# The last two rows of the last chunk but one, stored by indirect transfers from GpSimd

## The chip, the cores and the metric

The kernel runs on one core of a Trainium2 chip. The time is device microseconds of one execution. Before the change the median of three runs is 1331.59 us (1331.28 to 1331.63). A profile is one execution recorded on the chip.

## The reference

`logits` has shape (2, 8, 2112, 2112), `rel_bias` (8, 33), both float32.

```python
pos = np.arange(S)
rel = pos[:, None] - pos[None, :]
rel_clipped = np.clip(rel, -max_rel, max_rel) + max_rel        # max_rel = 16
bias = rel_bias[:, rel_clipped]
logits = logits + bias[None, :, :, :]
logits = logits - logits.max(axis=-1, keepdims=True)
exp = np.exp(logits)
return exp / exp.sum(axis=-1, keepdims=True)
```

A bias that depends only on the clipped distance between row and column is added, and a softmax is taken along each row of 2112. The input is 285 MB and so is the output.

## The kernel before

The 2 x 8 x 2112 = 33,792 rows are laid over the 128 partitions, 264 neighbouring rows to each. A chunk is six rows of every partition (`R = 6`), 128 x 50,688 bytes; there are 44 chunks, numbered 0 to 43 here, and four buffers `X[0]` to `X[3]` (`NBUF = 4`), used in turn. Chunk 42, the last but one, lies in `X[2]`.

At the start a table `M` of the bias against distance is built in PSUM; `strip` copies the stretch of it that four chunks need into `F`. For each row of a chunk VectorE adds the bias and finds the negated maximum (`add`, L181), ScalarE takes the exponential and its sum (`exps`, L190), and VectorE takes the reciprocals of three rows and scales them (`scale`, L198 and L202), in place. Each engine runs its own loop over chunks, and semaphores tie them: `ld[b]` says that buffer b is loaded, `scaled` counts rows that are done, `st[b]` that the store has landed. `take` waits for a count and takes it off again.

All big transfers are issued by SP, in one queue (q1 in the profile). Its loop stores a chunk when six rows of it are scaled (`store`, L93), waits until the store of the buffer before has landed, and loads the next chunk there (`load`, L89). A transfer of 128 partitions is spread over the core's 16 DMA engines, eight partitions to each.

Chunk 0 is stored in another way. Its first five rows go as one transfer (L219). The sixth goes as 17 small ones, the "fan" (L223), with 15, 14, 13, ... 1 partitions, which cover the 128 partitions between them. A transfer of k ≤ 15 partitions puts one on each of k DMA engines, so the fan loads them unequally. GpSimd waits for all of these (`main`, `fan[0]`, `fan[1]`) and then sets `st[0]`, which SP awaits in its loop.

After the loop SP stores chunks 41 and 42 whole and chunk 43 in two halves of three rows (semaphore `landed`). It waits for the remaining `st` and, at the very end of the program (L244), for `landed`.

Of the kernel before, what the change touches and what calls it, by code (L numbers as in the profile page):

```python
# [8 lines left out]
I32 = mybir.dt.int32  # L9
EXP = mybir.ActivationFunctionType.Exp  # L10
ALU = mybir.AluOpType
# [4 lines left out]
def kernel(  # L16
# [6 lines left out]
    nc = tc.nc  # L23
    P = 128
    B, H, S, S2 = logits.shape
# [3 lines left out]
    ROWS = B * H * S // P  # L29
    PB = S // ROWS  # L30
    assert ROWS * P == B * H * S and PB * ROWS == S and PB == H == 8
    R = 6
    NBUF = 4
    STEP = R * NBUF
    N = ROWS // R
# [2 lines left out]
    MW = S + ROWS - 1  # L38
    FW = S + STEP - 1
    BIG = 3.0e38  # L40
    LANES = 9
    FAN = []
    for lane in range(LANES):
        m = len(range(lane, P, LANES))
        k = 15 if lane == 0 else 15 - lane
# [4 lines left out]
    io = ctx.enter_context(tc.tile_pool(name="io", bufs=1))  # L50
    X = [io.tile([P, R * S], FP32, tag=f"X{b}", name=f"X{b}") for b in range(NBUF)]
# [2 lines left out]
    nmax = io.tile([P, STEP], FP32, tag="nmax", name="nmax")  # L54
    tot = io.tile([P, STEP], FP32, tag="tot", name="tot")
    rec = io.tile([P, STEP], FP32, tag="rec", name="rec")
    ip = io.tile([P, 3, PB], I32, tag="ip", name="ip")
    ps = ctx.enter_context(tc.tile_pool(name="ps", bufs=1, space=bass.MemoryType.PSUM))
    M = ps.tile([P, 4096], FP32, tag="M", name="M")

    def view(t, offset, dims):

        return bass.AP(tensor=t.tensor, offset=t.offset + offset, ap=[[list(t.ap[0])[0], P]] + dims)

    def rows(t, j, n):

        return bass.AP(tensor=t.tensor, offset=t.offset + j * S, ap=[[ROWS * S, P], [1, n * S]])

    with tc.tile_critical(no_gpsimd_drain=True):
        ld = [nc.alloc_semaphore(f"ld{b}") for b in range(NBUF)]  # L70
        st = [nc.alloc_semaphore(f"st{b}") for b in range(NBUF)]
        added = nc.alloc_semaphore("added")
        expd = nc.alloc_semaphore("expd")
        scaled = nc.alloc_semaphore("scaled")
# [2 lines left out]
        pre = nc.alloc_semaphore("pre")  # L77
        idx = nc.alloc_semaphore("idx")
        dve = nc.alloc_semaphore("dve")
        main = nc.alloc_semaphore("main")  # L80
        fan = [nc.alloc_semaphore(f"fan{i}") for i in range(2)]
        landed = tc.alloc_semaphore("landed")

        def take(eng, sem, n):
            eng.wait_ge(sem, n).then_inc(sem, -n)  # L85


        def load(j, b):
            nc.sync.dma_start(out=X[b][:, :], in_=rows(logits, j, R)).then_inc(ld[b], 16)  # L89

        def store(j, b, s0=0, n=R, sem=None):
            take(nc.sync, scaled, n)
            nc.sync.dma_start(  # L93
                out=rows(out, j + s0, n), in_=X[b][:, s0 * S : (s0 + n) * S]
            ).then_inc(sem or st[b], 16)


        for r in range(R):
            nc.sync.dma_start(
                out=X[0][:, r * S : (r + 1) * S], in_=rows(logits, r, 1)  # L100
            ).then_inc(ld[0] if r == R - 1 else pre, 16)
        for n in range(1, NBUF):
# [6 lines left out]
            out=rbB,  # L109
            in_=bass.AP(tensor=rel_bias.tensor, offset=rel_bias.offset, ap=[[0, P], [1, H * W]]),  # L110
        ).then_inc(rb, 16)
        nc.gpsimd.iota(ip[:, 0], pattern=[[0, PB]], base=0, channel_multiplier=1).then_inc(idx, 1)
        nc.gpsimd.iota(ip[:, 2], pattern=[[1, PB]], base=0, channel_multiplier=0).then_inc(idx, 1)  # L113
        take(nc.gpsimd, main, 16)
        take(nc.gpsimd, fan[0], 16 * ((len(FAN) + 1) // 2))
        take(nc.gpsimd, fan[1], 16 * (len(FAN) // 2))
        nc.gpsimd.sem_inc(st[0], 16)

        v = nc.vector
        done = [0]  # L120
# [21 lines left out]
        for m, op in ((eq, ALU.is_equal), (gt, ALU.is_gt), (le, ALU.is_le), (lt, ALU.is_lt)):  # L142
# [4 lines left out]
            out=view(F, 0, [[W, H], [1, W]]), in0=view(F, 0, [[W, H], [1, W]]),  # L147
# [3 lines left out]
                             axis=mybir.AxisListType.X, op=ALU.add))  # L151
# [5 lines left out]
            out=view(F, 0, [[W, PB], [1, W]]), in0=view(F, SC + 2 * PB, [[1, PB], [0, W]]),  # L157
# [7 lines left out]
            out=view(M, U, [[ROWS, PB], [1, W]]), in0=view(F, 0, [[W, PB], [1, W]]),  # L165
            in1=view(F, SC + 8 * PB, [[1, PB], [0, W]]), op=ALU.add))
        then(v.tensor_copy(out=view(M, U + W, [[ROWS, PB], [1, ROWS - W]]),  # L167
                           in_=view(F, SC + 7 * PB, [[1, PB], [0, ROWS - W]])))
# [8 lines left out]
        def add(b):  # L177
            take(v, ld[b], 16)
            for r in range(b * R, (b + 1) * R):
                x = X[b][:, (r - b * R) * S : (r - b * R + 1) * S]  # L180
                v.tensor_tensor_reduce(  # L181
                    out=x, in0=x, in1=F[:, STEP - 1 - r : STEP - 1 - r + S], scale=-1.0, scalar=BIG,
                    op0=ALU.add, op1=ALU.min, accum_out=nmax[:, r : r + 1],
# [37 lines left out]
        for i, (k, g, lane) in enumerate(FAN):  # L221
            p = g * LANES + lane
            nc.sync.dma_start(  # L223
                out=bass.AP(
                    tensor=out.tensor, offset=out.offset + (p * ROWS + R - 1) * S,
                    ap=[[LANES * ROWS * S, k], [1, S]],
                ),
                in_=bass.AP(
                    tensor=X[0].tensor, offset=X[0].offset + p * PSX + (R - 1) * S,
                    ap=[[LANES * PSX, k], [1, S]],  # L230
                ),
            ).then_inc(fan[i % 2], 16)
        with nc.Fori(0, ROWS - 2 * STEP + 1, STEP, engines=[ENG.SP]) as j:
            for b in range(NBUF):
                store(j + (b + 1) * R, (b + 1) % NBUF)
                take(nc.sync, st[b], 16)
                load(j + (b + NBUF) * R, b)
        for n in range(N - NBUF + 1, N - 1):
            store(n * R, n % NBUF)
        store((N - 1) * R, (N - 1) % NBUF, 0, HALF, landed)  # L240
        store((N - 1) * R, (N - 1) % NBUF, HALF, R - HALF, landed)
        for b in range(NBUF - 1):
            take(nc.sync, st[(N + b) % NBUF], 16)
    nc.sync.wait_ge(landed, nc.sync.to_reg(32), synchronizes=[nc.sync.lower_ap(out)])  # L244


# [28 lines left out]
```

## Time and profile before

| | |
|---|---|
| median of three runs | 1331.59 us |
| profiled execution | 1331.3 us |
| its span, first to last instruction | 1329.5 us |
| VectorE busy | 976.7 us, 73% |
| ScalarE busy | 575.2 us, 43% |
| GpSimd busy | 0.4 us |
| bytes moved | 285.61 MB read, 285.47 MB written, 430 GB/s over the span |

The page divides the span into 40 slices and gives each engine's busy tenths; the DMA row is the mean of the core's 16 DMA engines. A view of stretches gives the same between any two times. In it the last two numbers of a row are the DMA share and the GB/s, and the one before them is the granted clock of TensorE, which this kernel doesn't use. Issue times of transfers stand in the timeline of SP, with a q behind the engine's name for its queue of issues; when a transfer lands is given as a median by kind.

### The profile page before, as it was taken

To read this page: it belongs to the slowest core of one execution; us is meant where nothing else is said; L and a number is where in the kernel's file an instruction comes from. 1 tells how busy PE (TensorE), PEld (TensorE's weight loads), DVE (VectorE), ACT (ScalarE), POOL (GpSimd) and SP (SyncE) were. 2 spreads that over 40 slices of the span, in tenths; PEclk is the share of its full clock that TensorE was granted. 3 is DMA by queue.
4 is the path that set the end of the run, shared out by engine and by line. 5 is a ranking of instruction groups with operands and counts; after the bars stand their busy time and mean duration, and the time that the engine had idled before them with its cause. 6 is when DMAs were issued, how large, how long until landed. Compare 5 with 4: busy or idle time off the path is not lost. (4 is left out here: it accounts for less than half of the span.)

```text
span 1329.5 us, 2477 instructions
## 1 busy us (share of the span) xinstructions
DVE 976.7 (73%) x911; ACT 575.2 (43%) x539; POOL 0.4 (0%) x6
## 2 busy tenths in 40 slices
DVE  5998767777877776787778767677877776687772
ACT  2565333444444343345444333444444343345440
POOL 0000000000000000000000000000000000000000
DMA  9999999999999999999999999999999999999997
GB/s 391 427 426 424 436 430 433 438 433 435 432 435 435 433 436 430 436 433 435 430 433 439 433 433 427 439 435 432 433 432 438 430 433 430 436 430 436 438 432 337
DMA packets 13939, 571.12 MB, mean 430 GB/s; under 512 B 1648, under 2 KB 1776, under 8 KB 1776
## 3 DMA queue, kind: packets, MB, share of 16 engines
q1 hardware_dynamic: 13792, 570.96, 99.5%
q10 hardware_dynamic: 144, 0.14, 0.1%
q14 instruction: 3, 0.02, 0.0%
HBM read 285.61 MB, written 285.47 MB: 430 GB/s over the span
## 5 line engine op out<-in xcount | busy, mean ns | idle before, releaser
L181 DVE CUSTOM_DVE_ANT_0 X<-X,F 128x2112 f32<-128x2112 f32 x264 | 605.2, 2354 | 302.0 <-DVEq L85 302.0
L190 ACT ACTIVATE X<-X,nmax 128x2112 f32<-128x2112 f32 x264 | 541.7, 2052 | 538.2 <-ACTq L85 516.4
L202 DVE TENSOR_SCALAR X<-X,rec 128x2112 f32<-128x2112 f32 x264 | 332.5, 1316 | 13.2
L190 ACT ACT_TABLE_LOAD x11 | 14.1, 1283 | 185.8 <-ACTq L85 185.8
L190 ACT ACTIVATION_READ_ACCUMULATOR X<-X,nmax 128x1 f32 x264 | 49.2, 186 | 0.0
L175 DVE COPY F<-M 128x2135 f32 x11 | 26.1, 2375 | 6.6 <-DVEq L85 6.6
L181 DVE DVE_READ_ACCUMULATOR2_ANT nmax<- 128x1 f32 x264 | 21.7, 82 | 0.0
L198 DVE RECIPROCAL rec<-tot 128x3 f32<-128x3 f32 x88 | 15.0, 170 | 0.0
L146 DVE TENSOR_TENSOR F<-F 128x264 f32<-128x264 f32 x1 | 0.4, 435 | 4.9 <-DMA F<-in_rel_bias_dram 4.9
L167 DVE COPY M<-F 128x1848 f32<-128x1848 f32 x1 | 2.1, 2077 | 0.0
L133 DVE TENSOR_SCALAR ip<-ip 128x8 int32<-128x8 int32 x1 | 0.2, 172 | 1.3 <-POOL ip L113 1.3
L150 DVE TENSOR_REDUCE rbS<-F 128x33 f32<-128x264 f32 x1 | 0.6, 610 | 0.0
L164 DVE TENSOR_TENSOR M<-F 128x264 f32<-128x264 f32 x1 | 0.4, 441 | 0.0
L156 DVE TENSOR_TENSOR F<-F,rbS 128x264 f32<-128x264 f32 x1 | 0.4, 426 | 0.0
L143 DVE TENSOR_SCALAR F<-F 128x8 f32<-128x8 f32 x4 | 0.4, 167 | 0.0
L169 DVE COPY M<-rbS 128x247 f32<-128x247 f32 x1 | 0.4, 406 | 0.0
L154 DVE TENSOR_SCALAR F<-F,rbS 128x8 f32<-128x8 f32 x1 | 0.2, 231 | 0.0
L160 DVE SCALAR_TENSOR_TENSOR F<-F,rbS 128x8 f32<-128x8 f32 x1 | 0.2, 227 | 0.0
L155 DVE TENSOR_SCALAR F<-F,rbS 128x8 f32<-128x8 f32 x1 | 0.2, 225 | 0.0
L161 DVE SCALAR_TENSOR_TENSOR F<-F,rbS 128x8 f32<-128x8 f32 x1 | 0.2, 221 | 0.0
L136 DVE TENSOR_TENSOR F<-ip 128x8 f32<-128x8 int32 x1 | 0.2, 167 | 0.0
L139 DVE TENSOR_TENSOR F<-ip 128x8 f32<-128x8 int32 x1 | 0.2, 167 | 0.0
(9 smaller groups left out, 1.2 us busy)
## 6 DMA issues: line engine op xcount, KB each, us to landing
X<-in_logits_dram SPq DMA_DIRECT2D x43, 6336.0 KB, 44.7
out_dram<-X SPq DMA_DIRECT2D x42, 6336.0 KB, 52.8
X<-in_logits_dram SPq DMA_DIRECT2D x6, 1056.0 KB, 12.6
out_dram<-X SPq DMA_DIRECT2D x2, 3168.0 KB, 21.9
out_dram<-X SPq DMA_DIRECT2D x1, 5280.0 KB, 34.9
F<-in_rel_bias_dram ACTq DMA_DIRECT2D x1, 132.0 KB, 6.4
out_dram<-X SPq DMA_DIRECT2D x1, 123.8 KB
out_dram<-X SPq DMA_DIRECT2D x1, 115.5 KB
```

The lines of the kernel that those rows point to most:

```text
L143: then(v.tensor_scalar(out=m, in0=dp, scalar1=0.0, scalar2=None, op0=op))
L146: then(v.tensor_tensor(out=view(F, 0, [[W, H], [1, W]]), in0=view(F, 0, [[W, H], [1, W]]), in1=view(F, SC + 3 * PB, [[1, H], [0, W]]), op= ...
L150: then(v.tensor_reduce(out=rbS[:, :], in_=view(F, 0, [[1, W], [W, H]]), axis=mybir.AxisListType.X, op=ALU.add))
L156: then(v.tensor_tensor(out=view(F, 0, [[W, PB], [1, W]]), in0=view(F, SC + 2 * PB, [[1, PB], [0, W]]), in1=view(rbS, W - 1, [[0, PB], [-1, ...
L164: then(v.tensor_tensor(out=view(M, U, [[ROWS, PB], [1, W]]), in0=view(F, 0, [[W, PB], [1, W]]), in1=view(F, SC + 8 * PB, [[1, PB], [0, W]] ...
L167: then(v.tensor_copy(out=view(M, U + W, [[ROWS, PB], [1, ROWS - W]]), in_=view(F, SC + 7 * PB, [[1, PB], [0, ROWS - W]])))
L169: then(v.tensor_copy(out=M[:, 0:U], in_=low.to_broadcast([P, U])))
L175: v.tensor_copy(out=F[:, :], in_=M[:, bass.ds(ROWS - STEP - j, FW)]).then_inc(dve, 1)
L181: v.tensor_tensor_reduce(out=x, in0=x, in1=F[:, STEP - 1 - r : STEP - 1 - r + S], scale=-1.0, scalar=BIG, op0=ALU.add, op1=ALU.min, accum_ ...
L190: nc.scalar.activation(out=x, in_=x, func=EXP, scale=-1.0, bias=nmax[:, r : r + 1], accum_out=tot[:, r : r + 1],).then_inc(expd, 1)
L198: v.reciprocal(out=rec[:, r0 : r0 + HALF], in_=tot[:, r0 : r0 + HALF]).then_inc(inv, 1)
L202: v.tensor_scalar_mul(out=x, in0=x, scalar1=rec[:, r : r + 1]).then_inc(scaled, 1)
```

## The change

SP's store of chunk 42 is cut to its first four rows (`R - PAIR`). The last two rows of every partition, 2 x 2112 x 4 = 16,896 bytes that are neighbours in memory, are stored by GpSimd in six indirect transfers. Seen so, `out` is a table of 16,896 such pairs, and partition p's pair of chunk 42 has number 132 p + 128.

`PLAN` lists the six as (n, p0, a, b). Each transfer reads n partitions from p0 on, and takes its n targets from a column of the new tile `sel`. The column holds the pair numbers of partitions p0 to p0 + n - 1, with those outside the kept range a to b - 1 replaced by a number past the end of `out` (`FAR`), which an indirect transfer with `oob_is_err=False` skips. The kept ranges cover 0 to 127 once. The six lists name 16 + 16 + 16 + 48 + 48 + 112 = 256 partitions and keep 128.

GpSimd fills the columns at the start with 6 iotas and 12 selects, each waiting for the one before through the semaphore `pool`. It issues the transfers after a wait for `ready`, which SP sets when it has counted the six scaled rows of chunk 42, just ahead of its own shorter store. They count on the semaphore `soft`, awaited at the end of the program ahead of `landed`.

```diff
+    PLAN = [(16, 1, 12, 17), (16, 10, 17, 20), (16, 20, 20, 24), (48, 0, 0, 12), (48, 6, 24, 51), (112, 16, 51, 128)]
+    PAIR = 2
+    FAR = 1 << 20
...
+    sel = io.tile([P, len(PLAN)], I32, tag="sel", name="sel")
...
+        g = nc.gpsimd
+        BLK = ROWS // PAIR
+        AT = ((N - 1) * R - PAIR) // PAIR
...
+        for w, (n, p0, a, b) in enumerate(PLAN):
+            col = sel[:, w : w + 1]
+            step(g.iota(col, pattern=[[0, 1]], base=p0 * BLK + AT, channel_multiplier=BLK))
+            for base, mul in ((p0 - a, 1), (b - 1 - p0, -1)):
+                g.wait_ge(pool, made[0])
+                step(g.affine_select(out=col, in_=col, pattern=[[0, 1]], base=base, channel_multiplier=mul,
+                                     compare_op=ALU.is_ge, fill=float(FAR)))
+        take(g, pool, made[0])
         take(nc.gpsimd, main, 16)
         take(nc.gpsimd, fan[0], 16 * ((len(FAN) + 1) // 2))
         take(nc.gpsimd, fan[1], 16 * (len(FAN) // 2))
         nc.gpsimd.sem_inc(st[0], 16)
+        take(g, ready, 1)
+        pairs = out.rearrange("b h s t -> (b h s t)").rearrange("(n c) -> n c", c=PAIR * S)
+        late = X[(N - 2) % NBUF]
+        lap = list(late.ap[0])[0]
+        for w, (n, p0, a, b) in enumerate(PLAN):
+            g.indirect_dma_start(
+                out=pairs, out_offset=bass.IndirectOffsetOnAxis(ap=sel[0:n, w : w + 1], axis=0),
+                in_=bass.AP(tensor=late.tensor, offset=late.offset + p0 * lap + (R - PAIR) * S,
+                            ap=[[lap, n], [1, PAIR * S]]),
+                in_offset=None, bounds_check=B * H * S // PAIR - 1, oob_is_err=False,
+            ).then_inc(soft, 16)
...
-        for n in range(N - NBUF + 1, N - 1):
+        for n in range(N - NBUF + 1, N - 2):
             store(n * R, n % NBUF)
+        take(nc.sync, scaled, R)
+        nc.sync.sem_inc(ready, 1)
+        nc.sync.dma_start(
+            out=rows(out, (N - 2) * R, R - PAIR), in_=X[(N - 2) % NBUF][:, 0 : (R - PAIR) * S]
+        ).then_inc(st[(N - 2) % NBUF], 16)
...
+    nc.sync.wait_ge(soft, nc.sync.to_reg(16 * len(PLAN)), synchronizes=[nc.sync.lower_ap(out)])
     nc.sync.wait_ge(landed, nc.sync.to_reg(32), synchronizes=[nc.sync.lower_ap(out)])
```

More of the change, by code (lines that the diff above doesn't have):

```diff
@@ L40 @@
     BIG = 3.0e38
+    PLAN = [(16, 1, 12, 17), (16, 10, 17, 20), (16, 20, 20, 24), (48, 0, 0, 12), (48, 6, 24, 51), (112, 16, 51, 128)]
+    PAIR = 2
+    FAR = 1 << 20
+    assert sorted(p for n, p0, a, b in PLAN for p in range(a, b)) == list(range(P))
     LANES = 9
@@ L79 @@
         dve = nc.alloc_semaphore("dve")
+        ready = nc.alloc_semaphore("ready")
+        pool = nc.alloc_semaphore("pool")
+        soft = tc.alloc_semaphore("soft")
         main = nc.alloc_semaphore("main")
@@ L113, with step @@
         nc.gpsimd.iota(ip[:, 2], pattern=[[1, PB]], base=0, channel_multiplier=0).then_inc(idx, 1)
+        g = nc.gpsimd
+        BLK = ROWS // PAIR
+        AT = ((N - 1) * R - PAIR) // PAIR
+        made = [0]
+        def step(ins):
+            made[0] += 1
+            ins.then_inc(pool, 1)
+        for w, (n, p0, a, b) in enumerate(PLAN):
[6 more added lines that the diff above has]
+        take(g, pool, made[0])
         take(nc.gpsimd, main, 16)
```

## The prediction

> **What bounds the kernel.** The page first: its span, busy lines, slices and queues.
>
> ```profile
> span 1329.5 us, 2477 instructions
> DVE 976.7 (73%) x911; ACT 575.2 (43%) x539; POOL 0.4 (0%) x6
> DMA  9999999999999999999999999999999999999997
> ...
> q1 hardware_dynamic: 13792, 570.96, 99.5%
> q10 hardware_dynamic: 144, 0.14, 0.1%
> q14 instruction: 3, 0.02, 0.0%
> ```
>
> VectorE works 73% of the span and ScalarE 43%, but the DMA row reads nine tenths or more in 39 slices and 7 in the last. One queue, SP's q1, carries 99.5% of 16 engines' span. The kernel moves 571 MB as fast as its 16 DMA engines take it; only the start and that last slice leave them idle. The second view is stretches of time, for the DMA share (next to last column) and the GB/s.
>
> ```profile
> 78.00:1300.00 1222.00, 907.90 (x836) 538.82 (x506) 0.00 (x0) 1.00 1.00 433
> ...
> 1320.00:1321.00 1.00, 0.00 (x0) 0.00 (x0) 0.00 (x0) 1.00 0.77 329
> 1321.00:1322.00 1.00, 0.00 (x0) 0.00 (x0) 0.00 (x0) 1.00 0.59 253
> 1322.00:1323.00 1.00, 0.00 (x0) 0.00 (x0) 0.00 (x0) 1.00 0.41 177
> 1323.00:1324.00 1.00, 0.00 (x0) 0.00 (x0) 0.00 (x0) 1.00 0.41 177
> 1324.00:1325.00 1.00, 0.00 (x0) 0.00 (x0) 0.00 (x0) 1.00 0.24 101
> 1325.00:1326.00 1.00, 0.00 (x0) 0.00 (x0) 0.00 (x0) 1.00 0.18 76
> 1326.00:1327.00 1.00, 0.00 (x0) 0.00 (x0) 0.00 (x0) 1.00 0.06 25
> 1327.00:1328.00 1.00, 0.00 (x0) 0.00 (x0) 0.00 (x0) 1.00 0.06 25
> 1328.00:1329.50 1.50, 0.00 (x0) 0.00 (x0) 0.00 (x0) 1.00 0.00 0
> ```
>
> The share falls in sixteenths: three DMA engines at 1325, one alone (0.06) from 1326 to 1328. From 78 to 1300 us each engine moved 433 / 16 = 27.1 GB/s; the one left alone moves 25 by packets that start in the stretch, so no faster. The limit is per engine, and the time is set by the engine with the most left. The shares from 1320 on sum to 2.72 us of all sixteen. A packet counts where it starts, and one of 25,344 B lasts 0.94 us at 27.1 GB/s, so half of that is added: evenly shared, the work would end at 1320 + 2.72 + 0.47 = 1323.2. The last packet ends at 1328.1. **At most 4.9 us can be won by sharing the tail out.** Third, what the tail waits for: SP's waits, its issues, and the transfers by line (last column: median us from issue to landing).
>
> ```profile
> SPq L244 <- DMA out_dram<-X: 14.6, 1, 14.6
> ...
> 1238.15 0.35 SPq L89 DMA_DIRECT2D X<-in_logits_dram  x1
> 1244.93 60.38 SPq L93 DMA_DIRECT2D out_dram<-X  x4
> ...
> X<-in_logits_dram SPq DMA_DIRECT2D x43, 6336.0 KB, 44.7
> out_dram<-X SPq DMA_DIRECT2D x42, 6336.0 KB, 52.8
> out_dram<-X SPq DMA_DIRECT2D x2, 3168.0 KB, 21.9
> ```
>
> SP's last wait is for stores alone. A chunk's store lands 52.8 us after its issue though moving it takes 6.49 MB / 433 GB/s = 15 us: the queue is long, and a store issued a few us later starts no later.
>
> **Which DMA engine is late.** No view names engines. I followed the single packet records behind these rows: on one engine a packet starts a few ns before its predecessor ends. The fan of chunk 0 labels them, taking k ≤ 15 rows a transfer: engine 0 gets 17 rows, 1 to 6 get 15, 14, 13, 12, 11, 10, down to none on 15, against 8 if even. So read, the last packets end: engine 4 at 1328.1, engines 0 to 3 at 1324.6 to 1326.2, engine 5 at 1324.2, 6 to 8 at 1321.7 to 1322.3, the others at 1320.9 to 1322.0, save one at 1324.1, which I read as 10 or 15 and cannot settle. Engine 4 is no heir of the fan alone; its packets run about 0.4% long all through.
>
> **The change, part by part.**
>
> *The dealing.* Chunk 42 loses two of six rows from SP's store. They go as 128 pieces (two rows of a partition, 16,896 B), 16,896 / 27.1 = 0.62 us each. Before, each engine had 8. I take a list of n rows to be dealt in blocks of n/16: 7, 3 or 1 to an engine. Every kept range begins and ends on such a block (51 - 16 = 35 = 5 x 7; 24 - 6 = 18 = 6 x 3; 12 = 4 x 3). That gives engines 0 to 3 four pieces, 4 none, 5 seven, 6 and 10 ten, 7 to 9 and 11 to 14 eleven, 15 eight. Engine 4: -8 x 0.62 = -5.0, end 1323.1. Engines 0 to 3: -2.5, ends 1322.1 to 1323.7. Engine 5: -0.6, 1323.6. Engine 6: +1.25, 1323.6. Those with eleven: +1.9, 1322.8 to 1323.8. The odd one, if 15, stays at 1324.1; if 10, it goes to 1325.3. I take 15, since then all sixteen come within 2 us. Latest 1324.1 for 1328.1: **-4.0 us** (bounds -4.3 and -2.8).
>
> *Smaller pieces and six more completions per engine.* 11 pieces and 6 tokens at a few ns: +0.1 us.
>
> *Two queues on one DMA engine.* Before has no indirect transfer. The nearest rows are the start, where ACT's q10 (1,056 B packets) runs between SP's packets:
>
> ```profile
> 4.00:5.50 1.50, 0.00 (x0) 0.00 (x0) 0.00 (x0) 1.00 0.91 234
> 5.50:7.00 1.50, 0.00 (x0) 0.00 (x0) 0.00 (x0) 1.00 0.94 363
> 7.00:9.50 2.50, 2.00 (x7) 0.00 (x0) 0.00 (x0) 1.00 1.02 433
> ```
>
> Mixed with the first reads, the rate is 234, but in the packet records from 5.6 to 6.7 us single q10 packets of 47 ns stand between q1 packets at their usual 319 ns: 0 to 0.04 us a change. The other end is q14's instruction packet at 1310.6, behind which a q1 packet took 0.28 us too long. I take 0.02 x 11 = +0.2 us, nearest to two data queues; the upper end is 0.28 x 11 = 3.1.
>
> *Generation on GpSimd.* `ready` comes when chunk 42 is scaled:
>
> ```profile
> 1271.08 3.78 DVE L202 TENSOR_SCALAR X<-X,rec 128x2112 f32<-128x2112 f32 x3
> 1283.08 2.36 DVE L181 CUSTOM_DVE_ANT_0 X<-X,F 128x2112 f32<-128x2112 f32 x1 [8.22 <-DVEq L85]
> ...
> 1301.09 3.78 DVE L202 TENSOR_SCALAR X<-X,rec 128x2112 f32<-128x2112 f32 x3
> ...
> 44.01 12.37 SPq L223 DMA_DIRECT2D out_dram<-X  x17
> ```
>
> That is 1274.9; the queue is busy until 1320. Generation has 45 us of cover. SP's 17 small transfers issued in 12.4 us, so six take at least 6 x 0.73 = 4.4 us there; no row bounds GpSimd from above. I cost it at nothing; past the cover each us counts. The rows mostly land where SP's store did, so chunk 43's load (issued 1238.15, awaited at 1283.08) may be pushed by about a piece or two (1.2 us). Its first store half is issued when the run of 1297.08 ends, at 1300.9, and chunk 42's store lands only about 1306; cover 3 us, nothing on the path.
>
> *The lists.* 6 iotas and 12 selects on GpSimd at the start, before its wait for the first stores:
>
> ```profile
> 1.13 0.14 POOL L113 IOTA ip<- 128x8 int32 x1
> ...
> 19.04 2.38 DVE L175 COPY F<-M 128x2135 f32 x1 [6.58 <-DVEq L85]
> ```
>
> 18 x 0.14 plus a semaphore each is about 6 us; the wait behind them opens only at 78 us (the fan is issued at 44 to 56). [...] Nothing.
>
> *The ends.* SP waits for `soft` ahead of `landed`: the rows were issued 26 us before the last store, nothing. `soft` lies apart from the other cleared semaphores, so GpSimd clears twice; the whole stretch after the last packet is 1.4 us (1328.1 to 1329.5), one clear more +0.2 (bounds 0 and 1).
>
> Sum: -4.0 + 0.1 + 0.2 + 0.2 = **-3.5 us**. The profiled execution took 1331.3 (1.8 around its span): 1327.8. The median of the runs is 0.3 higher, 1331.59, so **1328.1**.
>
> [...]
>
> **Rivals.**
>
> 1. *The dealing is another* (piece i on engine i mod 16, or skipped pieces closed up before dealing). Modulo gives 7 to 9 pieces everywhere, engine 4 still 8, and the end stays: 1331.6 + 0.5 = 1332.1. For it: no list of before shows how GpSimd deals. Against: the ranges fall on blocks.
> 2. *Changing queues costs as behind q14.* 0.28 us a piece: engines 7 to 14 at up to 1323.8 + 3.1 = 1326.9, a gain of 1.2 less 0.3: 1330.7. From 0.37 us a piece nothing is left.
> 3. *Skipped pieces move all the same (slower).* The lists name 256 pieces and keep 128. If a skipped one occupies its engine like a kept one, each engine carries 16 for 8: +8 x 0.62 = 5.0 us, engine 4 too: 1331.6 + 5.0 + 0.5 = 1337.1. It decides once a skipped piece costs 0.45 of a kept one, since engine 4 skips sixteen (16 x 0.62 x 0.45 = 4.5, back at 1327.6). Nothing in before speaks for or against.
> 4. *GpSimd is late.* VectorE scales from 1297.08 to 1304.9. If generation cannot work beside VectorE and misses the 8.22 us gap, the last list (7 pieces, 4.4 us an engine) comes after 1305: still hidden. Only past about 1318 does it cost: at 1325, 1325 + 4.4 + 1.4 = 1330.8 of span, about 1333. [...]
>
> **How the numbers follow.** Forecast 0.56: the blocks account for every bound in the plan and the ends meet. Rival 1: 0.12 (0.09 within, 0.03 slower). Rival 2: 0.12 (0.10 within, 0.02 slower). Rival 3: 0.11. Rival 4: 0.05 (0.01 within, 0.04 slower). A setup cost that no row here shows: 0.04 slower. A change under 0.2%, 2.7 us, can hardly be told from none. Faster 0.56, same 0.20, slower 0.24. The forecast's own range is 1327.0 (nearly the whole 4.9 us) to 1329.5 (10 late, changes at 0.1 us). For 8 in 10 it reaches over rivals 1, 2 and part of 4, to 1333.5.
>
> **What would show it.** The end of the tail: shares staying near 1.0 until about 1322 and gone by 1324.5. q1 short of 2.16 MB, which another queue carries. Bytes unchanged (else rival 3). GpSimd's six transfers issued between 1275 and 1290. Wrong would be one engine alone for 2 us again (rival 1), or a share below 1 while both queues have work (rival 2).

## The result, and the profile after

The change made the kernel slower: 1337.38 us, the median of five runs (1336.70 to 1337.63), against 1331.34 us for the kernel before in runs beside it (1331.28 to 1331.63). The ratio is 1.0044, with a 95% interval from 1.0030 to 1.0059. The prediction was 1328.1 us in a range from 1327.0 to 1333.5. The profiled execution took 1336.7 us with a span of 1334.9, against 1331.3 and 1329.5 before: 5.4 us to account for.

The page of the changed kernel, its span, engines and queues, then the bytes of HBM:

```profile
span 1334.9 us, 2526 instructions
DVE 976.7 (73%) x911; ACT 575.2 (43%) x539; POOL 8.6 (1%) x30
...
q1 hardware_dynamic: 13792, 568.79, 98.8%
q0 software_dynamic: 352, 2.16, 0.6%
...
HBM read 285.61 MB, written 287.64 MB: 429 GB/s over the span
```

VectorE and ScalarE do what they did. GpSimd's queue q0 carries the 2.16 MB that q1 gave up, so the queues move 570.95 MB, the same as before. Yet the counter of HBM has 2.17 MB more written; an experiment below deals with that. q0 has 352 packets, 22 for each DMA engine, where 128 pieces were kept: the rest are packets of 4 bytes.

What GpSimd did, by its timeline (start, length):

```profile
1276.06 0.98 POOL L148 DMA_INDIRECT out_dram<-X,sel  x1 [1270.25 <-POOLq L93]
1277.34 0.86 POOL L148 DMA_INDIRECT out_dram<-X,sel  x1 [0.30 <-issue]
...
1282.03 0.94 POOL L148 DMA_INDIRECT out_dram<-X,sel  x1 [0.31 <-issue]
```

The six lists were written between 1276.1 and 1283.0, about 1 us each. By the packet records the first piece started at 1281.3 and the last of the six transfers was through by 1323.7. So neither GpSimd nor its queue is what ended last. The tail, in stretches of time (the last two columns are the DMA share and the GB/s):

```profile
1280.00:1300.00 20.00, 16.50 (x16) 12.89 (x12) 2.36 (x3) 1.00 1.00 389
1300.00:1320.00 20.00, 4.99 (x5) 0.00 (x0) 0.00 (x0) 1.00 0.98 364
1320.00:1324.00 4.00, 0.00 (x0) 0.00 (x0) 0.00 (x0) 1.00 1.01 429
1324.00:1326.00 2.00, 0.00 (x0) 0.00 (x0) 0.00 (x0) 1.00 0.80 342
1326.00:1329.00 3.00, 0.00 (x0) 0.00 (x0) 0.00 (x0) 1.00 0.33 144
1329.00:1333.00 4.00, 0.00 (x0) 0.00 (x0) 0.00 (x0) 1.00 0.06 25
1333.00:1335.00 2.00, 0.00 (x0) 0.00 (x0) 0.00 (x0) 1.00 0.00 0
```

The same stretches of the kernel before, as far as the prediction did not show them:

```profile
1280.00:1300.00 20.00, 16.77 (x16) 12.89 (x12) 0.00 (x0) 1.00 1.00 433
1300.00:1320.00 20.00, 4.72 (x5) 0.00 (x0) 0.00 (x0) 1.00 0.98 421
```

Read the last two columns together. From 1280 to 1320 the engines are as busy as before (1.00 and 0.98), but they move 389 and 364 GB/s for 433 and 421. In this count an engine with a packet in hand is busy even while the packet moves slowly (one of 16,896 B took 3825 ns, for a median of 629). Bytes missing: 20 us x (44 + 57) GB/s = 2.0 MB, which at 433 GB/s is 4.7 us of all sixteen engines.

The same comes out at the end. The shares from 1320 on sum to 4 x 1.01 + 2 x 0.80 + 3 x 0.33 + 4 x 0.06 = 6.87 us, so evenly shared the work would have ended at 1320 + 6.87 + 0.47 = 1327.3, where the same sum gave 1323.2 before. The last data packet ended at 1333.0, so 5.7 us are lost to uneven ends (4.9 before). The end of the program after it took 1.9 us instead of 1.4. **The work became 4.1 us longer for every engine, its ends became 0.8 us less even, and the program's end added 0.5.**

The packet records say which packets became long. Of those that start after 1262 us, I summed what each took above the median of its size (629 ns for 16,896 B, 940 for 25,344 B, 1251 for 33,792 B, 1872 for 50,688 B). Before, that is 0.5 us in all. After, it is 71.4 us, or 4.5 us an engine: 38.1 in GpSimd's 128 pieces (mean 926 ns, longest 3825), and 33.4 in SP's own packets (a 33,792 B packet took up to 5131). Followed engine by engine as the prediction did, the engine with no piece at all also has 3.7 us of such excess (0.5 before) and ended at 1326.6. The last one, at 1333.0, is an engine with eleven pieces: they took 1298 ns in the mean, and its excess is 10.4 us. The first list reads five neighbouring partitions, 12 to 16, on five engines at once. Of the first five pieces to start (they need not all be of that list) three took 3825, 3414 and 2385 ns, the other two 1058 and 629.

### The profile page after: what moved, and what is told of

Same layout as the page of the kernel before. It is cut to its first block, busy times and chain, and to the rows that moved or that the text cites. A ratio compares the mean times of both kernels' runs of the same rounds, so it can differ in the third digit from the quotient of the medians.

```text
span 1334.9 us, 2526 instructions
## 1 busy us (share of the span) xinstructions
DVE 976.7 (73%) x911; ACT 575.2 (43%) x539; POOL 8.6 (1%) x30
## 2 busy tenths in 40 slices
DMA packets 14291, 571.12 MB, mean 428 GB/s; under 512 B 1872, under 2 KB 2000, under 8 KB 2000
## 3 DMA queue, kind: packets, MB, share of 16 engines
q0 software_dynamic: 352, 2.16, 0.6%
## 5 line engine op out<-in xcount | busy, mean ns | idle before, releaser
L226 ACT ACT_TABLE_LOAD x11 | 14.1, 1283 | 186.0 <-ACTq L93 186.0
L148 POOL DMA_INDIRECT out_dram<-X,sel x6 | 5.4, 898 | 1271.8 <-POOLq L93 1270.2
```

What stands on the lines that cost most here:

```text
L148: g.indirect_dma_start(out=pairs, out_offset=bass.IndirectOffsetOnAxis(ap=sel[0:n, w : w + 1], axis=0), in_=bass.AP(tensor=late.tensor, of ...
L226: nc.scalar.activation(out=x, in_=x, func=EXP, scale=-1.0, bias=nmax[:, r : r + 1], accum_out=tot[:, r : r + 1],).then_inc(expd, 1)
```

## The experiments

Two theories stood at the start. *Queue:* a second queue, indirection, skipped entries or small pieces cost time on every engine. *Reading side:* call the engine that carries a partition in a transfer of 128 partitions its home engine, and a piece that another engine carries a foreign piece. A foreign piece meets the home engine, or other pieces, where SBUF is read, and both wait; in transfers of 128 partitions nothing meets. That was my supposition, and the expectations call it P and speak of a shared way out of SBUF. Both theories give excess in pieces and in SP's packets. All diffs are against the changed kernel; each batch had its own runs of the kernel before, with medians from 1331.43 to 1331.55.

### Two queues, indirection, skipping

**One list, nothing skipped** (ident):

```diff
-    PLAN = [(16, 1, 12, 17), (16, 10, 17, 20), (16, 20, 20, 24), (48, 0, 0, 12), (48, 6, 24, 51), (112, 16, 51, 128)]
+    PLAN = [(128, 0, 0, 128)]
```

> One indirect list of all 128 partitions, none skipped, instead of the six lists. The pieces, their queue and the time of issue stay; the skipped entries and the unequal dealing go. Three theories for the 6 us. P (reading side): pieces taken by another DMA engine than the one that carries these partitions in SP's transfers meet that engine, and other pieces, on a shared way out of SBUF; if this list is dealt as SP's transfers are, each engine reads its own partitions: 1331.3 + 0.6 for the longer end of the program = 1332, and 16,896-byte pieces at their clean 0.63 us. If it is dealt in another way, pieces are long again. Q (two queues): every piece of the second queue costs beside q1: about 4.5 us more, 1336. S (skipped entries move data, as the HBM counter's extra 2.16 MB suggests): nothing skipped, 1332, and HBM written back at 285.47 MB.

1331.55 us, ratio 1.0001 (0.9992 to 1.0011). All 128 pieces took 629 ns (longest 645), SP's packets 0.5 us above their medians in sum. Its stretches:

```profile
1280.00:1300.00 20.00, 15.42 (x15) 12.42 (x11) 0.00 (x0) 1.00 0.99 427
1300.00:1320.00 20.00, 6.08 (x6) 0.47 (x2) 0.00 (x0) 1.00 0.99 428
```

The rate stays. **The same pieces from the same queue cost nothing when each lies on the engine that the 128-partition deal gives it.**

**Without lists** (direct): a plain GpSimd transfer of the same rows.

```diff
-        for w, (n, p0, a, b) in enumerate(PLAN):
-            g.indirect_dma_start(
...
+        g.dma_start(out=rows(out, (N - 1) * R - PAIR, PAIR), in_=late[:, (R - PAIR) * S : R * S]).then_inc(soft, 16)
```

> GpSimd stores the two rows of all 128 partitions by one plain transfer: no list, no skipped entry, no indirection; same bytes, same second queue, same time of issue. P: 1332, if a plain transfer of 128 partitions is dealt alike from both queues. Q: about 1336, pieces long as after the change. S: 1332 and HBM written 285.47 MB.

1331.56 us, ratio 1.0001 (0.9991 to 1.0011), pieces 629 ns: the same.

**All entries skipped** (allskip): the six lists hold only the number past the end, and SP stores chunk 42 whole.

```diff
-            step(g.iota(col, pattern=[[0, 1]], base=p0 * BLK + AT, channel_multiplier=BLK))
+            step(g.iota(col, pattern=[[0, 1]], base=FAR, channel_multiplier=0))
...
-            out=rows(out, (N - 2) * R, R - PAIR), in_=X[(N - 2) % NBUF][:, 0 : (R - PAIR) * S]
+            out=rows(out, (N - 2) * R, R), in_=X[(N - 2) % NBUF][:, :]
```

> SP stores chunk 42 whole again, and GpSimd issues the six lists with every entry out of range, so 256 entries are skipped and none is kept. P: 1331.3 + 0.6 = 1332. Q: 22 tiny packets on each engine beside q1 and no data: 1332 to 1333. S: twice the skipped entries of the change, so HBM written up by 4.33 MB and about 8 to 10 us: 1340 or more.

1332.09 us, ratio 1.0005 (0.9995 to 1.0014). Its page:

```profile
q0 software_dynamic: 352, 0.00, 0.0%
...
HBM read 285.61 MB, written 289.80 MB: 433 GB/s over the span
```

The queue moved nothing, and the time says so too, but the HBM counter rose by 4.33 MB, which is 256 skipped entries x 16,896 B. So the counter's 2.17 MB in the changed kernel are its 128 skipped entries, counted and not moved. The prediction's third rival gives nearly the measured time (1337.1) and is not what happened.

### The dealing alone, without GpSimd

These take all of the change's GpSimd part away. SP stores four rows of chunk 42 and then the last two by small transfers, each dealt one partition to an engine.

```diff
+        for p0, step, n in LISTS:
+            nc.sync.dma_start(
+                out=bass.AP(tensor=out.tensor, offset=out.offset + (p0 * ROWS + (N - 1) * R - 2) * S,
+                            ap=[[step * ROWS * S, n], [1, 2 * S]]),
+                in_=bass.AP(tensor=late.tensor, offset=late.offset + p0 * lap + (R - 2) * S,
+                            ap=[[step * lap, n], [1, 2 * S]]),
+            ).then_inc(soft, 16)
```

**Eight times 16 neighbours** (hw16c): `LISTS = [(16 * t, 1, 16) for t in range(8)]`

> No GpSimd. SP stores four rows of chunk 42 as one transfer and the last two as eight transfers of 16 neighbouring partitions (0 to 15, 16 to 31, ...), one partition to each of the 16 DMA engines. Dealing stays even, 8 pieces each, all in q1. P: 16 engines read 16 neighbouring partitions at once, so several share one way: pieces of 1 to 3 us instead of 0.63, the time up by 5 to 15 us, 1336 to 1346. Q and S: one queue, nothing skipped: 1331.5.

1337.74 us, ratio 1.0043 (1.0026 to 1.0060). Pieces took 1370 ns in the mean, up to 4951, in sum 94.8 us above 629 ns. All of it shows in one row, the stretch in which they move:

```profile
1300.00:1320.00 20.00, 4.85 (x5) 0.00 (x0) 0.00 (x0) 1.00 0.99 281
```

Share 0.99, 281 GB/s, one queue, no list. *Queue* is refuted, and the loss is in which engine takes which partition.

**Eight times 128 partitions, 528 columns** (cols8): eight small transfers too, but each dealt in the usual way.

```diff
+        for c in range(8):
+            nc.sync.dma_start(
+                out=bass.AP(tensor=out.tensor, offset=out.offset + ((N - 1) * R - 2) * S + c * 528,
+                            ap=[[ROWS * S, P], [1, 528]]),
+                in_=late[:, (R - 2) * S + c * 528 : (R - 2) * S + (c + 1) * 528],
+            ).then_inc(soft, 16)
```

> No GpSimd. The two rows as eight transfers in SP's queue as with 16 partitions each, but each of all 128 partitions and an eighth of the columns (2,112 bytes a piece), so every engine reads what it reads in any transfer of 128 partitions. P: 1331.5 + 0.5 for 56 more packets an engine: 1332. If several transfers of small pieces cost as such, whoever reads: 1337 to 1339, as with 16 partitions at strides of 8 or 9.

1332.19 us, ratio 1.0004 (0.9995 to 1.0014), though it has 1024 pieces of 86 ns (longest 102). Neither the number of transfers nor small packets are at fault.

**Which side: SBUF or HBM** (hw16x, hw16y, hw16s). The reads are 16 neighbours or t, t + 8, t + 16, ...; the targets likewise, in all other combinations. In hw16x and hw16y the last two rows of chunk 42 therefore land permuted in the output.

```diff
-        LISTS = [(16 * t, 1, 16) for t in range(8)]
+        LISTS = [(16 * t, 1, t, 8, 16) for t in range(8)]     # hw16x: read neighbours, write every eighth
+        LISTS = [(t, 8, 16 * t, 1, 16) for t in range(8)]     # hw16y: read every eighth, write neighbours
+        LISTS = [(t, 8, 16) for t in range(8)]                # hw16s: every eighth on both sides
```

> As the kernel with eight transfers of 16 neighbouring partitions, but each transfer's 16 rows go to where the rows of partitions t, t+8, ..., t+120 belong, so the two rows of chunk 42 land permuted in the output; what is read is as there, what is written is spread as with a stride of eight. If reading neighbours from SBUF costs the time (P): as that kernel, 1336 to 1338, with pieces of up to 4 or 5 us. If writing neighbours' rows, 2.2 MB apart in HBM, costs it (H): near the kernel before, up to 1333.

> The mirror image: each of the eight transfers reads partitions t, t+8, ..., t+120 and writes where the rows of 16 neighbours belong; the two rows land permuted in the output. P: at most two or so engines share a way out at a time, well under 6 us: 1331.5 to 1334, pieces mostly 0.63 us, few over 1.3. H: as the kernel with neighbours in both, 1336 to 1338.

> Partitions t, t+8, ..., t+120 both read and written to their own rows: against the run that read these and wrote where neighbours belong (1339.45) only the targets in HBM differ. P refined (a piece read away from home takes twice as long when its own engine stores, and the late engine has eight of them): again 1338 to 1340. H as a second cause (neighbours' rows in HBM): 1333 or less.

| | reads | writes | us | ratio | pieces: mean, longest ns | excess of all packets, us |
|---|---|---|---|---|---|---|
| hw16c | neighbours | neighbours | 1337.74 | 1.0043 (1.0026 to 1.0060) | 1370, 4951 | 106.0 |
| hw16x | neighbours | every eighth | 1337.49 | 1.0040 (1.0025 to 1.0056) | 1346, 4960 | 106.2 |
| hw16y | every eighth | neighbours | 1339.45 | 1.0059 (1.0044 to 1.0074) | 914, 2532 | 51.9 |
| hw16s | every eighth | every eighth | 1339.10 | 1.0058 (1.0042 to 1.0073) | 910, 2716 | 54.2 |

The pieces follow the read side (1370 and 1346 ns with neighbours, 914 and 910 with every eighth) and not the write side: the waiting belongs to the reading of SBUF. My expectation for hw16y, 1331.5 to 1334, was wrong, and instructive. The excess is half as large and the time is longer: the packets of the last engine say why. It had eight foreign pieces of 1230 ns in the mean, twice 629, as if each met one other reader, and 8.4 us of excess in all; the last packet ended 8.2 us later than before (1336.3 for 1328.1). A mean excess matters less than what falls on the engine that is late anyway.

**Nine transfers of every ninth partition** (hw9), chosen on a supposition of mine that no run shows, that no two partitions of one such transfer have the same home engine: `LISTS = [(t, 9, len(range(t, P, 9))) for t in range(9)]`

> The two rows as nine transfers of the partitions t, t+9, t+18, ... (15 or 14 of them), which is how the fan of chunk 0 takes its partitions; SP's queue alone. Engines 0 to 13 get nine pieces, 14 two, 15 none. P: the partitions of a transfer lie on different ways, pieces at 0.63 us, and engine 4, the last, has one more: +0.6, 1332.1. H or any cost of small transfers as such: 1335 or more, like the transfers of 16 neighbours.

1338.91 us, ratio 1.0050 (1.0035 to 1.0066), expected 1332.1: missed again, by the same oversight. The pieces' mean is 862 ns, but on the last engine they still take about 1240. Even if pieces of one transfer don't meet each other, as I supposed, they can meet the home engine, which is storing its own four rows of chunk 42 and all of chunk 43, or a piece of the next transfer; the records don't say which.

### Relieving the late engine

**One piece at a time** (one_by_one): only engine 4's eight pieces are moved, supposed to be those of partitions 16 to 19 and 48 to 51. They go first, each by a list of its own, to engines that end early; the other 120 go by three lists of 128.

```diff
+    PLAN = [(16, 3, 16, 17), (16, 6, 17, 18), (16, 9, 18, 19), (16, 7, 19, 20),
+            (16, 34, 48, 49), (16, 41, 49, 50), (16, 43, 50, 51), (16, 45, 51, 52),
+            (128, 0, 0, 16), (128, 0, 20, 48), (128, 0, 52, 128)]
```

> [...] If P holds and the pieces pass while engine 4 still loads chunk 43 (until about 1282.5), engine 4 ends 5 us earlier, the next late engines at 1326.2 set the end: -1.9 + 0.8 for the longer program end and the tiny packets: 1330.3. If the way out of SBUF that engine 4 uses is itself the limit, engine 4 waits as long as it was relieved: 1332. If unequal dealing as such costs: 1335 or more.

1330.58 us, ratio 0.9993 (0.9984 to 1.0002). Every piece took 629 ns. Engine 4 had no piece, so these eight are the partitions that a list of 128 deals to it; with 5.0 us less to do it ended at 1326.3 instead of 1328.1, still the last. Its packets of SP's queue have 3.7 us of excess where they had 0.5 before, so 3.2 of the 5.0 us came back. The time is near the 1330.3 expected if the pieces passed freely, but by luck: there engine 4 was to be 5 us earlier and others were to end last. Even one foreign reader at a time takes back most of what it relieves the home engine of: eight pieces of 0.63 us cost it 3.2 us. My estimate from the 1230 ns of hw16y's pieces against 629 is that two engines that read one home engine's partitions together move about as much as one; the 3.2 of 5.0 us do not contradict it.

### While the home engine is not reading

If that holds, a foreign piece is free only while its home engine does something else. Chunk 43's load, issued at 1238 and landed about 45 us later, occupies the engines from about 1268 to 1283 (estimated from its 6.49 MB at 433 GB/s, 15 us), and writes SBUF.

**Chunk 41's rows, in that time** (loadwin), and **the same lists, chunk 42 and the change's time** (latewin):

```diff
+    PLAN = [(16, 34, 40, 48), (16, 26, 32, 40), (16, 5, 16, 20), (16, 42, 48, 52),
+            (128, 0, 0, 16), (128, 0, 20, 32), (128, 0, 52, 128)]
...
-        AT = ((N - 1) * R - PAIR) // PAIR                      # loadwin alone, from here on
+        AT = ((N - 2) * R - PAIR) // PAIR
...
-        late = X[(N - 2) % NBUF]
+        late = X[(N - 3) % NBUF]
...
+            out=rows(out, (N - 3) * R, R - PAIR), in_=X[(N - 3) % NBUF][:, 0 : (R - PAIR) * S]
+        ).then_inc(st[(N - 3) % NBUF], 16)
+        take(nc.sync, st[(N - NBUF) % NBUF], 16)
+        nc.sync.sem_inc(ready, 1)
+        store((N - 2) * R, (N - 2) % NBUF)
```

> Unequal dealing once more, nearly the shares of the change (engine 4 none, 0 to 3 four each, 5 and 15 eight, 6 to 14 nine to eleven), but of chunk 41, and at another time: GpSimd starts when chunk 40's store has landed (about 1268), so that the first four lists, which hold all pieces read by an engine other than their own, pass while engines 0 to 4 load chunk 43 (1268 to 1281) and read nothing from SBUF. The rest goes by lists of 128. P with the refinement that a piece only costs where the partition's own engine is reading: end of the last packet near 1324.3, -4.0, +0.2 for tiny packets, +0.2 for the longer program end: 1327.9. If the unequal dealing itself or the second queue costs: 1335 or more. If the limit is the late engine itself in some other way: 1331.5.

> The same lists as in the run that starts with chunk 40's landing, but of chunk 42 and started when it is scaled (1275), as in the change: most foreign pieces pass while their own engines store. P: both lose, pieces of 1.2 us and more, the gain is eaten: 1331 to 1337, above the early start by 3 us at least. If the time of reading does not matter: the same as the early start, within 0.5.

loadwin 1331.72 us, ratio 0.9998 (0.9989 to 1.0008), its runs from 1329.4 to 1333.1; latewin 1333.76, ratio 1.0018 (1.0009 to 1.0027), its runs from 1331.0 to 1335.8. loadwin missed the 1327.9 expected; latewin lies in its range, but 2.0 us above loadwin and not 3. By the medians the time of reading is worth those 2 us (some of it, up to 0.5, may be the program's end, since loadwin has `soft` beside `landed` and latewin has not), but the gain over the kernel before is not there. The packets of loadwin show pieces of up to 2.9 us: these lists put four neighbours on four engines at once, which may meet one another whatever the home engine does (excess 14.6 us; latewin 31.2, though its profiled execution took 1331.03 us and loadwin's 1332.22, so these two sums don't explain the medians). Its lists also came late, beside VectorE's scaling:

```profile
1269.05 1.86 POOL L149 DMA_INDIRECT out_dram<-X,sel  x1 [1262.47 <-POOLq L94]
1271.21 2.47 POOL L149 DMA_INDIRECT out_dram<-X,sel  x1 [0.30 <-issue]
...
1275.84 0.85 POOL L149 DMA_INDIRECT out_dram<-X,sel  x1 [0.30 <-issue]
```

**Lists that don't put neighbours on different engines at once, in that time** (spread), and **the same lists late** (spreadlate). A list of 48 deals three neighbours to one engine, which reads them one after the other, so that fewer neighbours are read at once. spread takes chunk 41's rows as loadwin did; GpSimd passes some 17 us with 34 small iotas after `ready`, so that the pieces fall into the load. Both have `soft` beside `landed`.

```diff
+    PLAN = [(48, 14, 32, 52), (16, 3, 16, 18), (16, 5, 18, 20),
+            (128, 0, 0, 16), (128, 0, 20, 32), (128, 0, 52, 128)]
...
+        for i in range(34):                                    # spread alone
+            g.iota(pad[:, :], pattern=[[1, 240]], base=i, channel_multiplier=0).then_inc(pool, 1)
+            take(g, pool, 1)
```

> The shares of the change once more (engines 0 to 3 four pieces, 4 none, 5 and 15 eight, 6 to 11 eleven, 12 to 14 ten), but with two things apart from the change: a list of 48 from partition 14 gives each of seven engines three neighbours to read one after the other, so that few pieces meet, and the rows are of chunk 41, with GpSimd kept busy by 34 fillings of a scratch tile (some 17 us) so that the foreign pieces pass at about 1267 to 1280, while engines 0 to 4 load chunk 43. P (only meetings cost): nearly all pieces at 0.63 us, last packet at 1324.2 to 1324.5, 1328 in all. If a piece read away from home costs in itself: 1332 or more and long pieces. If the pacing misses the window by some us: 1329 to 1332.

> The same lists for chunk 42, started when it is scaled, so that they pass while engines 0 to 4 store. P: engines 0 to 4 and the readers delay each other and most of the relief is given back: 1330 to 1334, above the paced run by 2 us or more. If the window does not matter: the same as the paced run within 0.5.

spread: **1328.70 us** (1327.72 to 1329.97), ratio 0.9980 (0.9971 to 0.9989). It beats both kernels. Its stretches:

```profile
1280.00:1300.00 20.00, 16.41 (x16) 12.89 (x12) 0.00 (x0) 1.00 1.03 444
1300.00:1320.00 20.00, 5.08 (x5) 0.00 (x0) 0.00 (x0) 1.00 0.97 415
1320.00:1324.00 4.00, 0.00 (x0) 0.00 (x0) 0.00 (x0) 1.00 0.62 266
1324.00:1326.00 2.00, 0.00 (x0) 0.00 (x0) 0.00 (x0) 1.00 0.09 38
1326.00:1329.00 3.00, 0.00 (x0) 0.00 (x0) 0.00 (x0) 1.00 0.00 0
```

All 128 pieces took 629 ns, the foreign ones from 1268.6 on, and all packets together are 1.5 us above their medians. The shares sum to 2.66, as little as before (2.72), and the last packet ends at 1325.3 instead of 1328.1; thirteen engines end between 1321.8 and 1323.6, three of those with eleven pieces at 1325.1 to 1325.3.

spreadlate: 1330.79 us, ratio 0.9995 (0.9986 to 1.0005). Its stretches where it differs:

```profile
1280.00:1300.00 20.00, 16.64 (x16) 12.89 (x12) 2.67 (x3) 1.00 0.98 410
1300.00:1320.00 20.00, 4.85 (x5) 0.00 (x0) 0.00 (x0) 1.00 1.00 425
1320.00:1324.00 4.00, 0.00 (x0) 0.00 (x0) 0.00 (x0) 1.00 0.71 302
```

The rate dips to 410 GB/s just when the foreign pieces move, SP's 50,688 B packets take up to 3324 ns, and the excess is 11.0 us, about 4.4 of it on engine 4, which ended at 1327.4. The lists name the same partitions in the same order; chunk and time differ. The 2.1 us between the two are, unless the chunk matters in another way, the price of reading a home engine's partitions while it reads them itself.

## Why the prediction was wrong

**What bounds the kernel: right.** The DMA engines were the bound, and their uneven ends can be won: spread won 2.8 of the 4.9 us in the last packet's end.

**The dealing: half right, and the step that failed.** "A list of n rows to be dealt in blocks of n/16" held to the piece: by the packet records one engine had none, four had four, then seven, eight, ten and eleven. (Two chains of the records can't be told apart between nine and thirteen pieces.) But the term "16,896 / 27.1 = 0.62 us each" took the piece's price from packets on their home engine and assumed it anywhere. In the changed kernel a piece cost 926 ns in the mean, and made SP's packets longer by nearly as much again (33.4 against 38.1 us). Two steps of the sum failed by it. "Engine 4: -8 x 0.62 = -5.0, end 1323.1": the engine without a piece ended at 1326.6, because other engines that read its partitions keep it waiting (one_by_one, with that relief alone: 3.2 of 5.0 us given back). "Those with eleven: +1.9, 1322.8 to 1323.8" set the time: one of them ended at 1333.0, with 10.4 us above what its packets take undisturbed. In the end of the last packet, -4.0 us became +4.9.

The prediction held a sentence that could have warned: "from 78 to 1300 us each engine moved 27.1 GB/s" names an engine's rate, and in all of that time each engine carried the eight partitions that a transfer of 128 gives it, so the rows could not tell whose limit it was. I wrote "The limit is per engine" without a row that separates them.

**Smaller pieces, two queues, the lists: right, and all nearly nothing.** ident carries the pieces, the second queue and one list, and has +0.1 us (-1.1 to +1.5) for a predicted 0.3; allskip carries all six lists and their completions, and has +0.6 (-0.7 to +1.9). The rival of 0.28 us a change of queue is refuted by ident: eight changes an engine would have shown as 2.2 us.

**Generation: right.** Six lists in 7 us beside 45 us of cover. That the last list ended at 1283.0, inside VectorE's gap, was owed to the early `ready`; beside VectorE's adds and scaling a list mostly took 1.6 to 2.7 us instead of 0.9, in loadwin above and in spread (one in latewin, at 1283.7, took 0.97 beside an add):

```profile
1263.09 2.32 POOL L153 DMA_INDIRECT out_dram<-X,sel  x1 [1.02 <-POOLq L95]
...
1275.97 0.96 POOL L153 DMA_INDIRECT out_dram<-X,sel  x1 [0.30 <-issue]
```

The rows show a slowing by about two to three times, and no run here shows its cause.

**The ends: mis-sized.** +0.2 predicted, +0.5 measured (1.4 to 1.9 us after the last packet); ident, with the same two clears, has 1.6 (1328.3 to 1329.9).

**The rivals.** Another dealing: refuted by the records. Changes of queue: refuted by ident. Skipped pieces that move: allskip refutes it, though its 1337.1 is close to what was measured; a time that fits is no evidence for its mechanism. GpSimd late: refuted by the timeline (the last list ended at 1283.0). That generation cannot work beside VectorE, as this rival supposed, no run shows: beside it lists took 1.6 to 2.7 us. What happened was none of the four, and the range's upper end, 1333.5, had no case behind it in which a piece takes longer because another engine reads it, or holds up the engine that it was taken from.

**What stays open.** Which partitions have the same home engine was supposed, and one_by_one bears it out for engine 4 alone: the engine without a piece there is the one on which all of the excess fell. How an engine's partitions are shared between readers is open too: in one_by_one the foreign pieces kept their 629 ns and only the home engine's packets grew. spread differs from spreadlate in the chunk as well as the time, since a chunk's rows can't be stored at the other's time. Why engine 4's packets run 0.4% long from the start was not looked into.

## What to carry to other kernels

Before moving a transfer's pieces from a late DMA engine to others, ask who else reads that engine's partitions at the time: here the reads by other engines gave back most of the relief (3.2 of 5.0 us), unless the home engine was loading at that time (1328.7 against 1330.8 us here for the same lists). Where the DMA share stays near 1 and the GB/s fall (0.99 and 281 in hw16c), the engines have work and their packets are waiting; here the cause was in who reads what. A rate read from traffic in which two things always go together (an engine and its eight partitions) belongs to neither until a run takes them apart.

## What the runs showed that I had not expected

- Skipped entries of an indirect transfer are counted by the HBM counter as written (4.33 MB for 256 in allskip, with 0.00 MB in the queue's row) and cost no time that could be measured (+0.6 us, from -0.7 to +1.9). In the records each is a packet of 4 bytes and 9 ns.
- From the end of the first list's generation (1277.0) to its first piece (1281.3) 4.3 us passed.
- Half the excess with a worse time (hw16y against hw16c): 51.9 us of excess, 8.4 of it on the engine that ends last, cost more than 106.0 spread over the engines (in hw16c all had ended by 1334.6, in hw16y the last at 1336.3).
